# A token mixer without GpSimd: low parts on VectorE, conditioning sums on TensorE, dt inside an exponent

## The chip, the cores and the metric

The kernel runs on one core of a Trainium2 chip. A core has TensorE (matrix products into PSUM), VectorE and ScalarE (elementwise work, both reach SBUF and PSUM), GpSimd (elementwise work on SBUF), SyncE (here the issuer of nearly all DMAs) and 16 DMA engines. In the profile they are PE (PEld for its weight loads), DVE, ACT, POOL and SP. Each engine works through its own queue in order; semaphores make one wait for another. The metric is the device time of one execution in microseconds (us).

## The reference

One encoder layer on 256 tokens of width 1024: a token mixer and a top-4-of-32 mixture of experts, each normalised before and after and modulated by a conditioning vector. Cut to what matters here:

```python
mod = silu(c) @ w_ada + b_ada                       # 6 x 1024: shift, scale, gate, twice
h = rmsnorm(res) * (1 + scale_m) + shift_m
proj = h @ w_in                                     # 1024 x 5664: q, k, v, z, xbc, dt
# 16 attention heads: three dilated windows, ALiBi, mixed by their softmax sums
attn = softmax(q k^T / 8 - slope * |i - j| + log(count of windows)) v
# SSD, 16 heads, forward and backward: xbc through a convolution over 5 tokens and silu
dt = softplus(dt_raw + dt_bias); a_cum = cumsum(dt * -exp(a_log))
y = (C B^T * exp(a_cum_l - a_cum_s) * dt_s, masked) @ xs + d_skip * xs
y = rmsnorm(y * silu(z))
res = res + gate_m * rmsnorm([attn, y] @ w_out)
# experts: 32 x (1024 x 2048 and 1024 x 1024), top 4 of each token
```

## The kernel before, in words

One function writes every engine's queue in program order; nothing is reordered behind it, so the order of the code is the order of each queue.

**Weights.** All weights come as 1 MB blocks through a ring of buffers (`RING`, 7 at first, more as other pools close), in one fixed list `loads`: 8 blocks of `w_ada` for the first modulation, then 22 blocks of `w_in` (256 columns each) with 16 further blocks of `w_ada` between them from the seventh on, 8 blocks of `w_out`, then 12 per expert. `consumed(i)` says that a block is no longer needed; its buffer then takes the next load, issued on SyncE's queue.

**Products in two parts.** The large products of the mixer are made with fp32 numbers split into a high part and a low part. `split(i, a)` does this for half a block (128 x 1024): ScalarE copies the half into `wh` (rounding it), then `wl = w - wh` (L383) is made, on GpSimd where `on_pool` says so (57 halves), else on VectorE (3). `ahead` calls it two halves before use. `mm3` then makes three matmuls, high by high, high by low, low by high. `unit` is one half block: 24 matmuls of 256 columns (L391).

**The projection loop** runs over n = 0 to 21, a block of `w_in` each, two units per n. The columns come in the order: six blocks for the convolution, four z, four q, then k and v in turn. After each unit stand the conditioning work (`mod_half`, from n = 5) and steps of a background list (`bg`), whose number `PACE` sets: the cumulative sums, then the SSD heads in eight pairs j (`ssd_bg`, from n = 7), then the attention heads in eight pairs (`att_bg`, from n = 14, as k and v arrive). A part of `bg` stands in the middle of a unit.

**Conditioning.** The other five rows of `mod` are eight groups of 512 columns. For each group VectorE multiplies 8 slices of `w_ada` (128 x 512) by a column of silu(c) and adds them up (`macc`, L354 and L356); then `mod_sum` sums over the partitions with four matmuls in a 128 x 32 form (L366), which put group g into row g of each quarter of a PSUM tile (`pssq`).

**SSD.** `ssd_decay(h)` builds a head's exponents in PSUM (L556 to L559: at each position the cumulative sum, plus a mask of -1e30), ScalarE takes exp with the bias `natok` (L563), and VectorE multiplies by dt and by C B^T (`cbm`, L565, four pieces per head: 256, 128, 128, 256 columns). `ssd_merge` adds forward and backward on the two diagonal blocks (L575), `ssd_out` multiplies with the inputs (L583), `ssd_fin` squares and splits the result (L593, L595).

**Attention.** `att_scores(j)` makes the scores of two heads (L640), VectorE adds the table of distances and takes the row maximum in one instruction (L652), L655 negates it, ScalarE takes exp and the row sums (L657). `att_norm(j)` divides by the sums (L664, L666 on VectorE), `att_T(j)` turns them (L680 on TensorE, L682), `att_out(j)` multiplies with v (L691). In `att_bg` the steps are: scores of j, normalising of j - 1 and output of j - 2, turning of j - 1.

**After the loop** come the output projection (16 halves of `w_out`, again `ahead` and `mm3`), beside it the splitting of the expert biases (`bias_parts`, L299, L300, loads `bgu` in four chunks), the router and the experts.

Of the kernel before, what the change touches and what calls it, by code (L numbers as in the profile page):

```python
# [40 lines left out]
MIXC = dict(le=128, ones=128, ge=128, dist=384, lnc=384)  # L41


def make_consts():
# [13 lines left out]
        dist=dist, lnc=np.where(count > 0, np.log(np.maximum(count, 1)), NEG))  # L58
# [16 lines left out]
def tile_hybrid_block(  # L75
# [136 lines left out]
    dist, lnc = mcx[:, 0:384], mcx[:, 384:768]  # L212
# [18 lines left out]
    one31 = mi.tile([P, 63], F32, name="one31")  # L231
    dve.memset(one31, 0.0)
    dve.memset(one31[:, 31:32], 1.0)
# [53 lines left out]
    act.activation(csT, colv[:, 0:8], AF.Silu)  # L287
    dve.tensor_copy(ident_b, ident)
# [56 lines left out]
    def mod_half(i, a):  # L345

        w = wt[W_MOD[i]].rearrange("p (k n) -> p k n", k=4)
        if i % 2 == 0 and a == 0:
            macc[i // 2] = mb.tile([P, 512], F32, name="macc", tag="macc", bufs=2)
        acc = macc[i // 2]  # L350
        for kk in range(2 * a, 2 * a + 2):
            k = 4 * (i % 2) + kk
            if k == 0:
                dve.tensor_scalar(acc, w[:, kk, :], csT[:, 0:1], None, op0=OP.mult)  # L354
            else:
                dve.scalar_tensor_tensor(acc, w[:, kk, :], csT[:, k:k + 1], acc, op0=OP.mult, op1=OP.add)  # L356
# [3 lines left out]
    macc = {}  # L360

    def mod_sum(g):

        acc = macc.pop(g)
        for b in range(4):
            pe.matmul(pssq[32 * b:32 * b + 32, 128:256], one31[:, 31 - g:63 - g], acc[:, 128 * b:128 * b + 128],  # L366
                      start=(g == 0), stop=True, tile_position=(0, 32 * b), skip_group_check=True)
# [7 lines left out]
    def on_pool(i, a):  # L375
        return W_IN[order[1]] <= i < W_OUT[6] or (i, a) == (W_OUT[6], 0)

    def split(i, a, pl=None, bufs=3):
# [4 lines left out]
        (pool if on_pool(i, a) else dve).tensor_sub(lo.bitcast(F32R), src, hi)  # L383
# [118 lines left out]
    def cumulate():  # L502
# [25 lines left out]
        dve.tensor_scalar(natok, pt2[:, 0:64].rearrange("p (t n) -> p t n", t=2), -1.0, None, op0=OP.mult)  # L528
# [16 lines left out]
    BLK = ((0, 256, 0, 0, 0), (384, 128, 1, 0, 128), (256, 128, 0, 1, 0), (512, 256, 1, 1, 0))  # L545
    mt = {}

    def ssd_decay(h):
# [82 lines left out]

    slopes = [2.0 ** (-8.0 * (h + 1) / HEADS) for h in range(HEADS)]
    pts = {}

    def att_scores(j):
# [8 lines left out]
        for q in range(2):  # L644
            h = 2 * j + q
            tb = mb.tile([P, 384], F32, name="tb", tag="tb", bufs=2)
            dve.scalar_tensor_tensor(tb, dist, -slopes[h], lnc, op0=OP.mult, op1=OP.add)
            sc = scs[:, 512 * q:512 * q + 512].rearrange("p (t k) -> p t k", t=2)
            st = mb.tile([P, 8], F32, name="st", tag="st", bufs=4)
            for t in range(2):  # L650
                o = 128 - 128 * t
                dve.tensor_tensor_reduce(out=sc[:, t, :], in0=pair[q][:, 256 * t:256 * t + 256],  # L652
                                         in1=tb[:, o:o + 256], scale=1.0, scalar=-3.0e38,
                                         op0=OP.add, op1=OP.max, accum_out=st[:, t:t + 1])
            dve.tensor_scalar(st[:, 2:4], st[:, 0:2], -1.0, None, op0=OP.mult)  # L655
            for t in range(2):
                act.activation(sc[:, t, :], sc[:, t, :], AF.Exp, bias=st[:, 2 + t:3 + t],  # L657
# [681 lines left out]
```

## Time and profile before

| | us |
|---|---|
| median of 3 runs | 1361.26 (1360.2 to 1363.12) |
| the profiled execution, its own time | 1363.41 |
| its span, first to last instruction | 1361.3 |
| start, to the second unit | 0 to 43.3 |
| first blocks: convolution, dt | 43.3 to 91.0 |
| n = 6, 7 | 91.0 to 115.7 |
| n = 8 to 13, SSD | 115.7 to 189.9 |
| n = 14, 15, SSD | 189.9 to 222.7 |
| n = 16 to 21, attention | 222.7 to 300.9 |
| output projection | 300.9 to 360.0 |
| norm, router, selection | 360.0 to 391.5 |
| experts and end | 391.5 to 1361.3 |

The stages are cut at the first matmul of a unit, or of the first expert. [...] A row of a wait names who waited for whose result. Busy time of VectorE includes the time in which a started instruction stands still.

### The profile page before, as it was taken

The numbers are of one execution on the slowest core, as the hardware profiler recorded it, in microseconds if no ns is written. First come the engines' busy times: TensorE is split into PE (matmuls) and PEld (weight loads), VectorE is DVE, ScalarE is ACT, GpSimd is POOL, SyncE is SP. The second block draws the span as 40 slices with busy tenths as digits, with TensorE's granted clock in tenths as the row PEclk, the third lists the DMA queues.
The fourth block names the chain that finished last, engine by engine and source line by source line (L and its number), as shares of the span: only waits on it lengthen the run. The fifth ranks groups of instructions, "written<-read, shape, count | busy, mean of one in ns | idle before, by whom it ended". The sixth has DMA issues, their size and how long they took to land. (4 is left out here: it accounts for less than half of the span.)

```text
span 1361.3 us, 16342 instructions
## 1 busy us (share of the span) xinstructions
PE 1174.9 (86%) x6394; PEld 587.1 (43%) x6394; DVE 456.7 (34%) x866; ACT 262.9 (19%) x582; POOL 168.6 (12%) x91
## 2 busy tenths in 40 slices
PE   3877776889879999999995999999998999999996
PEld 1776665676633333333342333333333333333332
DVE  0799998875711111211110111112111111111113
ACT  1645344543311000110010110001100001110001
POOL 0555443346300000000000000000000000000000
PEclk9889887989889999999997999999999899999998
DMA  8855644456669999999997999999999999999992
GB/s 312 258 175 194 196 155 136 162 184 267 264 248 413 414 413 415 414 414 413 413 417 306 415 415 413 415 413 415 414 413 409 415 415 414 416 415 413 413 385 101
DMA packets 113466, 465.96 MB, mean 342 GB/s; under 512 B 10955, under 2 KB 34163, under 8 KB 79507
## 3 DMA queue, kind: packets, MB, share of 16 engines
q1 hardware_dynamic: 112576, 462.39, 86.1%
q8 instruction: 106, 1.74, 0.5%
q10 hardware_dynamic: 723, 1.33, 0.3%
q14 instruction: 61, 0.50, 0.1%
HBM read 462.65 MB, written 1.05 MB: 341 GB/s over the span
## 5 line engine op out<-in xcount | busy, mean ns | idle before, releaser
L1118 PE MATMUL pq_u<-w,xg 128*64 128x512 f32 x1024 | 275.0, 595 | 2.1 <-issue 2.1
L1118 PE MATMUL pq_g<-w,xg 128*64 128x512 f32 x1024 | 274.5, 596 | 1.5 <-issue 1.0
L1156 PE MATMUL pq_u<-w,aT 128*64 128x512 f32 x1008 | 226.8, 595 | 2.3
L1129 DVE TENSOR_SCALAR g<-pq_g 128x512 f32<-128x512 f32 (+1 forms) x33 | 22.6, 683 | 474.7 <-PE pq_g L1118 271.1
L383 POOL TENSOR_TENSOR wl<-w,wh 128x1024 fp32r<-128x1024 f32 x57 | 145.6, 2560 | 137.9 <-ACT wh L382 133.1
L1130 ACT ACTIVATE sg<-g 128x512 f32<-128x512 f32 (+1 forms) x33 | 20.6, 623 | 723.4 <-DVE g L1129 701.4
L1118 PEld LDWEIGHTS pq_u<-w,xg 128*64 128x64 f32 x1024 | 77.5, 138 | 144.7 <-issue 142.5
L1118 PEld LDWEIGHTS pq_g<-w,xg 128*64 128x64 f32 x1024 | 76.8, 138 | 133.1 <-issue 120.1
L1156 PEld LDWEIGHTS pq_u<-w,aT 128*64 128x64 f32 x1008 | 70.6, 137 | 136.8 <-issue 124.2
L1228 DVE COPY y<-pq_u 128x512 f32<-128x512 f32 x31 | 21.5, 692 | 228.5 <-PE pq_u L1156 227.6
L391 PE MATMUL ps_pj<-hh,wh 128*128 128x256 f32 x296 | 94.0, 317 | 4.3 <-DVE hh L449 3.4
L391 PE MATMUL ps_pj<-hh,wl 128*128 128x256 f32 x296 | 89.9, 304 | 7.4 <-POOL wl L383 7.4
L391 PE MATMUL ps_pj<-hl,wh 128*128 128x256 f32 x296 | 89.7, 303 | 0.0
L827 POOL TENSOR_TENSOR rows<-kc,gp 128x1024 f32<-128x1024 f32 x1 | 1.9, 1895 | 699.9 <-PE o L1074 699.9
L356 DVE SCALAR_TENSOR_TENSOR macc<-w,csT,macc 128x512 f32<-128x512 f32 x56 | 80.9, 1445 | 1.3
L1039 PEld LDWEIGHTS pq_m<-sel,xt 128*128 128x128 f32 x544 | 64.8, 196 | 24.8 <-issue 24.0
L1039 PE MATMUL pq_m<-sel,xt 128*128 128x128 f32 (+1 forms) x544 | 71.0, 285 | 0.0
L1042 ACT ACTIVATE xg<-pq_m,modT,g 128x128 f32<-128x128 f32 x128 | 48.2, 456 | 108.2 <-PE pq_m L1039 108.2
L382 ACT ACTIVATE wh<-w 128x1024 fp32r<-128x1024 f32 x60 | 63.4, 1057 | 29.3 <-issue 8.5
L1167 PE MATMUL o<-y,sT 64*128 64x512 f32 x256 | 65.6, 615 | 1.6 <-DVE y L1304 1.6
L391 PEld LDWEIGHTS ps_pj<-hh,wh 128*128 128x128 f32 x296 | 62.7, 212 | 9.1 <-issue 7.6
L391 PEld LDWEIGHTS ps_pj<-hh,wl 128*128 128x128 f32 x296 | 62.3, 211 | 8.2 <-POOL wl L383 8.2
(302 smaller groups left out, 1148.5 us busy)
## 6 DMA issues: line engine op xcount, KB each, us to landing
w<-in_w_gate_up_dram SPq DMA_DIRECT2D x256, 1024.0 KB, 19.1
w<-in_w_down_dram SPq DMA_DIRECT2D x127, 1024.0 KB, 20.0
w<-in_w_ada_dram SPq DMA_DIRECT2D x24, 1024.0 KB, 5.2
w<-in_w_in_dram SPq DMA_DIRECT2D x22, 1024.0 KB, 13.6
w<-in_w_out_dram SPq DMA_DIRECT2D x8, 1024.0 KB, 5.0
xt<-in_x_dram ACTq DMA_DIRECT2D x1, 1024.0 KB
w<-in_w_down_dram SPq DMA_DIRECT2D x2, 512.0 KB
out_dram<-xt SPq DMA_DIRECT2D x4, 256.0 KB, 2.2
```

Source lines behind the costliest of these rows:

```text
L356: dve.scalar_tensor_tensor(acc, w[:, kk, :], csT[:, k:k + 1], acc, op0=OP.mult, op1=OP.add)
L382: act.activation(hi.bitcast(F32R), src, AF.Copy)
L383: (pool if on_pool(i, a) else dve).tensor_sub(lo.bitcast(F32R), src, hi)
L391: pe.matmul(out_ap, u, v, start=first and i == 0, stop=last and i == 2, skip_group_check=True)
L1039: pe.matmul(p[:, w * i:w * i + w], res[:, t, k * 128:(k + 1) * 128], sel[:, t], start=(t == 0), stop=(t == 1))
L1042: act.activation(xg[:, k], p[:, w * i:w * i + w], AF.Identity, bias=m_shift[:, k:k + 1], scale=g1[:, 8 + k:9 + k])
L1118: pe.matmul(dst[cs * q:cs * q + cs, 0:w], xg[:, k], weight(k, o, w), start=False, stop=(k == KD - 1), tile_position=(0, cs * q), skip_grou ...
L1129: dve.tensor_scalar(g, pg, 7.0, None, op0=OP.min)
L1130: act.activation(s, g, AF.Sigmoid, scale=1.702)
L1156: pe.matmul(py[cs * q:cs * q + cs, 0:w], a4[:, k % nj, k // nj, :], weight(KD + k, w * q, w), start=(k == 0), stop=(k == KD - 1), tile_pos ...
L1167: pe.matmul(oacc[t][hf], sT[64 * q:64 * q + 64, 128 * t:128 * t + 128], y[64 * q:64 * q + 64, :], start=False, stop=False, tile_position=( ...
L1228: dve.tensor_copy(y, py)
```

## The change

- `split`: every low part is made on VectorE; `on_pool` is gone.
- `mod_half`: the sums over `w_ada` are made on TensorE, straight from the weight block, 8 matmuls of 128 columns in the 128 x 32 form for each half block; `cs31` holds each column of silu(c) between zeros, so that the group's sums fall into its row. `macc`, `mod_sum` and their calls are gone; the block is released when TensorE has read it.
- `cumulate`: log(dt) is taken (at least 1e-37) and added to `natok`, so that exp(bias + ...) holds the factor dt. `ssd_decay` ends with the exponentials; `ssd_merge` adds the diagonal blocks and then multiplies by C B^T in one instruction of 512 columns.
- Attention: q is scaled by -0.125 and the table negated; the row minimum of the negated scores is the bias of the exponential, whose scale is -1; L655 is gone. `att_norm` multiplies on ScalarE.

```diff
+    cs31 = mi.tile([P, KD, 63], F32, name="cs31")
+    pool.memset(cs31, 0.0)
...
+    dve.tensor_copy(cs31[:, :, 31:32], csT[:, :, None])
...
     def mod_half(i, a):
...
-        acc = macc[i // 2]
+        g = i // 2
         for kk in range(2 * a, 2 * a + 2):
             k = 4 * (i % 2) + kk
-            if k == 0:
-                dve.tensor_scalar(acc, w[:, kk, :], csT[:, 0:1], None, op0=OP.mult)
-            else:
-                dve.scalar_tensor_tensor(acc, w[:, kk, :], csT[:, k:k + 1], acc, op0=OP.mult, op1=OP.add)
+            for b in range(4):
+                pe.matmul(pssq[32 * b:32 * b + 32, 128:256], cs31[:, k, 31 - g:63 - g], w[:, kk, 128 * b:128 * b + 128],
+                          start=(i == 0 and k == 0), stop=True, tile_position=(0, 32 * b), skip_group_check=True)
...
-        (pool if on_pool(i, a) else dve).tensor_sub(lo.bitcast(F32R), src, hi)
+        dve.tensor_sub(lo.bitcast(F32R), src, hi)
...
-        dve.tensor_scalar(natok, pt2[:, 0:64].rearrange("p (t n) -> p t n", t=2), -1.0, None, op0=OP.mult)
+        dve.tensor_scalar(natok, ddt[:, :, 0:32], 1e-37, None, op0=OP.max)
+        act.activation(natok, natok, AF.Ln)
+        dve.scalar_tensor_tensor(natok, pt2[:, 0:64].rearrange("p (t n) -> p t n", t=2), -1.0, natok,
+                                 op0=OP.mult, op1=OP.add)
...
-        for o, n, t, dr, lo in BLK:
-            dve.scalar_tensor_tensor(ee[:, o:o + n], ee[:, o:o + n], ddt[:, t, 16 * dr + h:16 * dr + h + 1],
-                                     cbm[:, h // 8, 256 * t + lo:256 * t + lo + n], op0=OP.mult, op1=OP.mult)
...
+        both = bass.AP(tensor=m.tensor, offset=m[:, 0:1].offset, ap=[list(m.ap[0]), [512, 2], [1, 256]])
+        dve.tensor_tensor(out=both, in0=both, in1=cbm[:, h // 8, :].rearrange("p (t n) -> p t n", t=2), op=OP.mult)
...
-            dve.scalar_tensor_tensor(tb, dist, -slopes[h], lnc, op0=OP.mult, op1=OP.add)
+            dve.scalar_tensor_tensor(tb, dist, slopes[h], nlc, op0=OP.mult, op1=OP.add)
...
-                                         in1=tb[:, o:o + 256], scale=1.0, scalar=-3.0e38,
-                                         op0=OP.add, op1=OP.max, accum_out=st[:, t:t + 1])
-            dve.tensor_scalar(st[:, 2:4], st[:, 0:2], -1.0, None, op0=OP.mult)
+                                         in1=tb[:, o:o + 256], scale=1.0, scalar=3.0e38,
+                                         op0=OP.add, op1=OP.min, accum_out=st[:, t:t + 1])
             for t in range(2):
-                act.activation(sc[:, t, :], sc[:, t, :], AF.Exp, bias=st[:, 2 + t:3 + t],
+                act.activation(sc[:, t, :], sc[:, t, :], AF.Exp, bias=st[:, t:t + 1], scale=-1.0,
                                accum_out=st[:, 4 + t:5 + t])
...
-                dve.tensor_scalar(sc[:, t, :], sc[:, t, :], st[:, 6 + t:7 + t], None, op0=OP.mult)
+                act.activation(sc[:, t, :], sc[:, t, :], AF.Copy, scale=st[:, 6 + t:7 + t])
...
-        if n > ADA_AT and (n - ADA_AT) % 2 == 0 and n - ADA_AT <= len(W_MOD):
-            mod_sum((n - ADA_AT) // 2 - 1)
```

On VectorE, in the SSD stage (one n; `ee` is a head's mask, `w_956` a conditioning block, `yt` the output of a pair), the queue before reads:

```order
L565 SCALAR_TENSOR_TENSOR ee<-ee,ddt,cbm 128x256
L565 SCALAR_TENSOR_TENSOR ee<-ee,ddt,cbm 128x128 x2
L565 SCALAR_TENSOR_TENSOR ee<-ee,ddt,cbm 128x256
L356 SCALAR_TENSOR_TENSOR macc<-w_956,csT,macc 128x512 x2
L565 SCALAR_TENSOR_TENSOR ee<-ee,ddt,cbm 128x256
L565 SCALAR_TENSOR_TENSOR ee<-ee,ddt,cbm 128x128 x2
L565 SCALAR_TENSOR_TENSOR ee<-ee,ddt,cbm 128x256
L575 TENSOR_TENSOR ee<-ee 128x2x128
L356 SCALAR_TENSOR_TENSOR macc<-w_956,csT,macc 128x512 x2
L586 SCALAR_TENSOR_TENSOR yt<-blk_c,dsk,ps_t 128x256
L587 TENSOR_TENSOR yt<-yt,blk_z 128x256
L575 TENSOR_TENSOR ee<-ee 128x2x128
```

and in the changed kernel, in the same stage (`w_1020` is a block of `w_in`, `wl` its low part):

```order
L368 TENSOR_TENSOR wl<-w_1020,wh 128x1024
L584 SCALAR_TENSOR_TENSOR blk_c<-yt,ghalf,blk_z 128x256
L561 TENSOR_TENSOR ee<-ee 128x2x128
L563 TENSOR_TENSOR ee<-ee,cbm 128x2x256
L368 TENSOR_TENSOR wl<-w_1020,wh 128x1024
L574 SCALAR_TENSOR_TENSOR yt<-blk_c,dsk,ps_t 128x256
```

The eight mask products and the conditioning products are gone; a low part stands before and behind the merge of a head, which now carries the product with C B^T.

On ScalarE, in the attention stage (`sc` are scores, `wh` the high part of a half block), before, from one pair's exponentials (L657) to the turned scores (L682):

```order
L382 ACTIVATE wh<-w_2007 128x1024
L682 ACTIVATE prT<-ps_t 128x512 x2
L657 ACTIVATE sc,st<-sc,st 128x256 x4
L739 ACTIVATE vt<-ps_pj 128x2x256
L382 ACTIVATE wh<-w_2149 128x1024
L694 ACTIVATE blk_q<-ps_pj 128x256
L682 ACTIVATE prT<-ps_t 128x512 x2
```

and after:

```order
L367 ACTIVATE wh<-w_2071 128x1024
L670 ACTIVATE prT<-ps_t 128x512 x2
L645 ACTIVATE sc,st<-sc,st 128x256 x4
L727 ACTIVATE vt<-ps_pj 128x2x256
L367 ACTIVATE wh<-w_2217 128x1024
L654 ACTIVATE sc<-sc,st 128x256 x4
L682 ACTIVATE blk_q<-ps_pj 128x256
L670 ACTIVATE prT<-ps_t 128x512 x2
```

Four normalising instructions (L654) now stand on ScalarE between a pair's exponentials and the copies of the turned scores.

On TensorE the eight matmuls of a conditioning half block now stand behind each unit, here between the last of its 24 matmuls and the output of an SSD pair:

```order
L376 MATMUL ps_pj<-hl,wh 128x256
L376 MATMUL ps_pj<-hh,wl 128x256
L352 MATMUL pssq<-w_986,cs_123 32x128 x8
L571 MATMUL ps_t<-ee,xtk 64x256 x4
L376 MATMUL ps_pj<-hh,wh 128x256
```

Before, four such matmuls from `macc` stood there once in two n.

## Rows read from the trace of the kernel before

**Rows 1.** Windows by stage: us, busy time by engine (instructions), PE clock, DMA share, GB/s

```profile
43.30:91.00 47.70, 41.01 (x326) 38.69 (x325) 38.38 (x57) 23.72 (x36) 28.99 (x14) 0.96 0.68 214
91.00:115.70 24.70, 16.55 (x122) 15.00 (x120) 24.45 (x35) 11.38 (x20) 10.98 (x5) 0.92 0.61 199
115.70:189.90 74.20, 57.98 (x452) 51.57 (x449) 73.60 (x109) 35.31 (x75) 37.76 (x18) 0.89 0.53 171
189.90:222.70 32.80, 24.44 (x173) 19.20 (x169) 30.29 (x48) 11.64 (x29) 12.59 (x8) 0.84 0.50 161
222.70:300.90 78.20, 64.54 (x465) 54.89 (x461) 61.36 (x146) 37.84 (x94) 30.67 (x12) 0.89 0.45 149
300.90:360.00 59.10, 49.87 (x237) 38.23 (x234) 39.41 (x60) 21.88 (x33) 35.45 (x17) 0.98 0.67 259
```

**Rows 2.** Single source lines: duration ns minimum/median/maximum, first and last start us, shapes

```profile
L356 DVE SCALAR_TENSOR_TENSOR macc<-w,csT,macc x56: 736/752/2935, 93.9 to 290.6; 128x512 f32<-128x512 f32 x56
L428 DVE SCALAR_TENSOR_TENSOR ctmp<-halo,colv,ctmp x48: 471/473/2650, 61.3 to 113.5; 128x256 f32<-128x256 f32 x48
L666 DVE TENSOR_SCALAR sc<-sc,st x32: 346/353/2534, 231.6 to 315.1; 128x256 f32<-128x256 f32 x32
L383 POOL TENSOR_TENSOR wl<-w,wh x57: 2375/2443/3012, 44.5 to 349.8; 128x1024 fp32r<-128x1024 f32 x57
L383 DVE TENSOR_TENSOR wl<-w,wh x3: 1201/1210/1225, 36.3 to 357.4; 128x1024 fp32r<-128x1024 f32 x3
```

**Rows 3.** Timeline near 50 us, GpSimd and VectorE: start us, us, what

```profile
50.38 2.42 POOL L383 TENSOR_TENSOR wl<-w,wh 128x1024 fp32r<-128x1024 f32 x1 [0.43 <-ACT wh L382]
50.50 2.39 DVE L483 SCALAR_TENSOR_TENSOR vt<-vt 128x64 f32<-128x64 f32 x1
```

**Rows 4.** Waits of TensorE, 43.3 to 360: us in total, times, longest us

```profile
PE ps_bc L556 <- ACT ee L563: 16.7, 12, 4.4
PE ps_t L680 <- DVE sc L666: 14.6, 5, 5.0
...
PE ps_bc L391 <- DVE wl L383: 4.4, 1, 4.4
```

**Rows 5.** Timeline near 260 us, VectorE and TensorE, idle time before in brackets

```profile
257.23 8.84 DVE L356 SCALAR_TENSOR_TENSOR macc<-w,csT,macc 128x512 f32<-128x512 f32 x4
271.02 1.94 PE L680 MATMUL ps_t<-kc,sc 128*128 128x128 f32 x8 [4.97 <-DVE sc L666]
```

**Rows 6.** Groups by line on VectorE, 0 to 400: busy us, mean ns | idle before

```profile
L356 DVE SCALAR_TENSOR_TENSOR macc<-w,csT,macc 128x512 f32<-128x512 f32 x56 | 80.9, 1445 | 1.3
L565 DVE SCALAR_TENSOR_TENSOR ee<-ee,ddt,cbm 128x256 f32<-128x256 f32 (+1 forms) x64 | 41.0, 702 | 0.6 <-ACT ee L563 0.6
L666 DVE TENSOR_SCALAR sc<-sc,st 128x256 f32<-128x256 f32 x32 | 15.8, 536 | 0.6
L300 DVE CAST bias<-bgu 96x512 bf16<-96x512 f32 (+2 forms) x12 | 12.9, 1074 | 9.4 <-DMA bgu<-in_b_gate_up_dram 9.1
L911 DVE TENSOR_TENSOR xtk<-xtk,gbm 128x512 f32<-128x512 f32 x4 | 2.7, 685 | 0.2 <-ACT junk L908 0.2
```

**Rows 7.** Timeline of TensorE around two sums over partitions (L366)

```profile
135.77 0.66 PE L366 MATMUL pssq<-macc,one 128*32 128x128 f32 x8
136.36 0.58 PE L391 MATMUL ps_pj<-hh,wh 128*128 128x256 f32 x1
276.64 0.42 PE L366 MATMUL pssq<-macc,one 128*32 128x128 f32 x8
277.00 0.39 PE L391 MATMUL ps_pj<-hh,wh 128*128 128x256 f32 x1
```

**Rows 8.** Groups by line on ScalarE: busy us, mean ns | idle before

```profile
L595 ACT ACTIVATE blk_z<-yt,ghalf 128x256 fp32r<-128x256 f32 x8 | 3.9, 492 | 0.0
L563 ACT ACT_TABLE_LOAD x1 | 1.3, 1283 | 0.0
```

**Rows 9.** Window at the first expert's first matmuls, columns as in rows 1

```profile
390.00:395.00 5.00, 3.52 (x12) 1.25 (x14) 0.00 (x0) 0.00 (x0) 0.00 (x0) 0.50 0.01 3
```

More of the change, by code (lines that the diff above doesn't have):

```diff
@@ L40 @@
 KEEPB = dict(lt=128, e3=NE, up=128, low=128)
-MIXC = dict(le=128, ones=128, ge=128, dist=384, lnc=384)
+MIXC = dict(le=128, ones=128, ge=128, dist=384, nlc=384)
 def make_consts():
@@ L57, in make_consts @@
         blk=row // 32 == np.arange(4)[None, :],
-        dist=dist, lnc=np.where(count > 0, np.log(np.maximum(count, 1)), NEG))
+        dist=dist, nlc=np.where(count > 0, -np.log(np.maximum(count, 1)), -NEG))
     def pack(names):
@@ L211, in tile_hybrid_block @@
     mcx = mb.tile([P, 768], F32, name="mcx")
-    dist, lnc = mcx[:, 0:384], mcx[:, 384:768]
+    dist, nlc = mcx[:, 0:384], mcx[:, 384:768]
     qT, kT, zT, cvx = {}, {}, {}, {}
@@ L230, in tile_hybrid_block @@
     arow = mi.tile([P, 32], F32, name="arow")
-    one31 = mi.tile([P, 63], F32, name="one31")
-    dve.memset(one31, 0.0)
-    dve.memset(one31[:, 31:32], 1.0)
+    cs31 = mi.tile([P, KD, 63], F32, name="cs31")
+    pool.memset(cs31, 0.0)
     dsk = mx.tile([P, 8], F32, name="dsk")
@@ L347, in mod_half @@
         w = wt[W_MOD[i]].rearrange("p (k n) -> p k n", k=4)
-        if i % 2 == 0 and a == 0:
-            macc[i // 2] = mb.tile([P, 512], F32, name="macc", tag="macc", bufs=2)
-        acc = macc[i // 2]
+        g = i // 2
         for kk in range(2 * a, 2 * a + 2):
             k = 4 * (i % 2) + kk
-            if k == 0:
-                dve.tensor_scalar(acc, w[:, kk, :], csT[:, 0:1], None, op0=OP.mult)
-            else:
-                dve.scalar_tensor_tensor(acc, w[:, kk, :], csT[:, k:k + 1], acc, op0=OP.mult, op1=OP.add)
+            for b in range(4):
+                pe.matmul(pssq[32 * b:32 * b + 32, 128:256], cs31[:, k, 31 - g:63 - g], w[:, kk, 128 * b:128 * b + 128],
+                          start=(i == 0 and k == 0), stop=True, tile_position=(0, 32 * b), skip_group_check=True)
         if a:
             consumed(W_MOD[i] + 1)
[L360 to L367, printed above, removed]
     ptx = [ps("bc", 2), ps("bc", 2), ps("pj", 3), ps("pj", 3)]
@@ L373, in tile_hybrid_block @@
             pe.transpose(ptx[k // 2][:, o:o + 128], xn[:, t, k * 128:(k + 1) * 128], ident)
-    def on_pool(i, a):
-        return W_IN[order[1]] <= i < W_OUT[6] or (i, a) == (W_OUT[6], 0)
     def split(i, a, pl=None, bufs=3):
@@ L541, in xs_tok @@
         act.activation(xtk[:, t, 512 * hf:512 * hf + 512], p, AF.Copy)
-    BLK = ((0, 256, 0, 0, 0), (384, 128, 1, 0, 128), (256, 128, 0, 1, 0), (512, 256, 1, 1, 0))
+    BLK = ((0, 256, 0, 0), (384, 128, 1, 0), (256, 128, 0, 1), (512, 256, 1, 1))
     mt = {}
@@ L560, in ssd_decay @@
         ee = big("ee")
-        for o, n, t, dr, lo in BLK:
+        for o, n, t, dr in BLK:
             src = 0 if n == 256 else 256
             act.activation(ee[:, o:o + n], pb[dr][:, src:src + n], AF.Exp, bias=natok[:, t, h + 16 * dr:h + 16 * dr + 1])
-        for o, n, t, dr, lo in BLK:
-            dve.scalar_tensor_tensor(ee[:, o:o + n], ee[:, o:o + n], ddt[:, t, 16 * dr + h:16 * dr + h + 1],
-                                     cbm[:, h // 8, 256 * t + lo:256 * t + lo + n], op0=OP.mult, op1=OP.mult)
         mt[h] = ee
@@ L752, in evac @@
                 qT[j + i] = blk("q")
-                dve.tensor_scalar(qT[j + i], v3[:, i], 0.125, None, op0=OP.mult)
+                dve.tensor_scalar(qT[j + i], v3[:, i], -0.125, None, op0=OP.mult)
             yield
```

## The prediction

> **What bounds the kernel now.** I read the table of stages first. The span has three parts: a start of 43 us that the loads pace, the token mixer up to about 391 us, and the 32 experts. Only the mixer is edited. In its input projection after the convolutions, 91.0 to 300.9 us, VectorE is busy 24.45 + 73.60 + 30.29 + 61.36 = 189.7 of 209.9 us, 90%; TensorE is idle 8.15 + 16.22 + 8.36 + 13.66 = 46.4 us and runs at a mean granted clock between 0.84 and 0.92 [rows 1]. [...]
>
> Why VectorE is full I read from minimum, median and maximum of single lines. The conditioning sum (L356) takes 752 ns in the median and 2935 at most, a convolution tap (L428) 473 and 2650; the longest exceed the median by about one GpSimd low part, 2443 ns [rows 2]. The timeline shows the mechanism: at 50.38 us GpSimd starts a low part of 2.42 us, at 50.50 VectorE starts an operation on 64 columns that ends only when the low part does, after 2.39 us [rows 3]. So an instruction of VectorE that meets a low part waits it out.
>
> Who waits for VectorE comes from the waits. TensorE waits 16.7 us for the exponentials of the SSD mask and 14.6 us for normalised attention scores [rows 4]. One case in full: four products of the conditioning sum hold VectorE from 257.23 for 8.84 us, the next scores come late, and TensorE stands 4.97 us before L680 at 271.02 [rows 5]. VectorE's backlog sets the mixer's pace, TensorE pays.
>
> **The change, part by part.** *Conditioning sums leave VectorE*: 56 products, 80.9 us of its time, of which 56 x 0.752 = 42 us is work and the rest waiting for GpSimd [rows 2, 6]. *The SSD mask*: 64 three-operand products, 41.0 us, become 16 plain products of 512 columns. The nearest row is L911 (512 columns, two SBUF inputs), 685 ns: 16 x 0.685 = 11.0 us [rows 6]. *Low parts come to VectorE*: 57 at the 1.21 us that three of them take there already, 69 us in all [rows 2]; between 91.0 and 300.9 us it is 32 (two for each of 16 steps), 38.7 us. VectorE's sum there: 189.7 - 80.9 - 41.0 + 38.7 + 11.0 = 117.5 us, 56% of the old stretch, before the blocked time on what stays is taken off. It stops being the bound.
>
> *Conditioning sums come to TensorE*: 32 half blocks of 8 matmuls each, which is two groups of four in the form of L366; L366 itself (8 groups) goes. A group takes 277.00 - 276.64 = 0.36 us from its start to the next matmul at full clock, 136.36 - 135.77 = 0.59 at half clock, the switch out of and into the 128 x 128 form included [rows 7]. So 64 - 8 = 56 groups add 20.2 us, or 33.0 if all fell at half clock. I take 20.2, since these groups stand right behind 24 matmuls of a unit, where the engine has been running. Nothing hides them: TensorE is in order. This is the price of the change. TensorE now also waits itself for each conditioning block's load; the DMA share of 0.45 to 0.61 in these stages [rows 1] leaves room, so I cost that at nothing; a late block would stop TensorE by as much as it is late.
>
> *Normalising goes to ScalarE*: 32 multiplications of VectorE (15.8 us, median 353 ns) become ScalarE instructions. The nearest row is L595, 256 columns with a per-partition scale, 492 ns: 15.7 us [rows 2, 6, 8]. ScalarE is busy 37.8 of 78.2 us in that stage [rows 1], so 24 of them (11.8 us) fit; but they now stand behind the exponentials of the next pair, in the chain scores, exponentials, normalising, transposes that already ends at L680. [...]
>
> *Small ones*: the logarithm of dt adds an instruction to VectorE, one to ScalarE and two table loads of 1.28 us [rows 8], once, between 60 and 91 us, where ScalarE is busy 23.7 of 47.7 us [rows 1]: 0, at most 3 us if the masks wait for it. The sign changes drop 16 tiny instructions; a GpSimd fill and a copy of 8 columns fall into the start, which loads pace.
>
> *Order.* Nothing is scheduled anew, but each low part now stands in VectorE's queue behind whatever waits there. In the projection it is wanted two units later, each 24 matmuls plus about 0.7 us of conditioning, so a wait of a few us is covered. Two places are tight. Near 50 us the dt chain now starts behind a low part (1.21 us, itself behind ScalarE's high part), and TensorE's transposes wait for that chain. In the output projection the bias casts (L300) wait 9.1 us for their DMA [rows 6], and low parts that GpSimd made meanwhile now queue behind them.
>
> **The sum**, stage by stage. 43.3 to 91.0: VectorE is busy 38.4 of 47.7 us, it gets some eleven low parts (13.3 us) and loses blocked time of about that size; I take 0, bounds -4 and +5 (idle is 6.7). 91.0 to 300.9: with VectorE at 56% I let 70% of the idle go, 32.5 us; the rest are latencies of chains such as the one before L680. The clock goes with the idle: the stages with the smallest idle share, 43.3 to 91.0 and 300.9 to 360.0, have 0.96 and 0.98 [rows 1]. All of the 48 us worked off at 2.4 GHz would give 24 us, I take 60%, 14.4. Less 20.2 for the new matmuls: 26.7. 300.9 to 360.0: of 9.2 us idle the 4.4 us wait for a late low part on VectorE goes [rows 4]; I take 4, bounds -5 (the bias DMA) and +9. Together 30.7, say 31 us.
>
> What the mixer gains, the experts pass on: weights stop arriving at 390 to 395 us (DMA share 0.01), because every ring buffer is full before the first expert's matmuls free one [rows 9]. The expert stage starts earlier with the same stock. The profiled execution took 1363.4 us, so it would be 1332; the runs' median is 2 us below it, and 1361.3 - 31 gives **1330**.
>
> **Rivals.** *(a) TensorE fully busy.* All 46.4 us idle and 24 us of slow clock go: 46.4 + 24 - 20.2 = 50 us, with 7 more from the ends: 1304. For it: VectorE and ScalarE both fall well under TensorE. Against: some waits are chains across four engines that no spare capacity shortens.
>
> *(b) The queue takes half back.* Low parts stand behind waiting instructions and normalising behind exponentials; only half of the idle and the slow clock go: 23 + 12 - 20 = 15 us, nothing at the ends: 1346. For it: 14.6 us of the waits are at L680, whose chain gets longer on ScalarE. Against: the longest of them is the conditioning sum's doing, and that is gone.
>
> *(c) Slower: TensorE is already the pacer and its new work is simply added.* If the waits are latencies rather than backlog, none goes, and 56 groups cost 20.2 us, at half clock 33: 1381 to 1394. It decides as soon as idle and slow clock give back less than 20 us together. Against it: VectorE's idle time in 115.7 to 189.9 us is 0.6 of 74.2 us, which is no latency. [...]
>
> *(d) No effect: the time is lost again before or in the expert stage.* An earlier start with an emptier ring would make the experts wait for weights at the end; 1361. Against: the loads stand still for several us before the first expert.
>
> **Numbers.** Forecast 0.55; (a) 0.16; (b) 0.17; (c) 0.06; (d) 0.06. The predicted time is that of the forecast. The range leaves out (c), (d) and the far half of (a): 1306 to 1350. Measurement can tell 0.2% (2.7 us) from no change: faster 0.89, same 0.05, slower 0.06.
>
> **What would show it.** VectorE's busy share in the projection near 55 to 60%, its products without a tail near 2.7 us, no GpSimd low parts; 64 groups of conditioning matmuls, 0.36 us each; TensorE idle there 10 to 18 us and granted clock about 0.95; experts' matmuls starting near 361 us instead of 391, and the last stage as long as before. I am wrong if TensorE still waits over 25 us there, if low parts on VectorE take clearly more than 1.21 us, or if the first expert starts earlier and the end does not.

## The result, and the profile after

The changed kernel takes 1320.3 us in the median (1319.6 to 1321.95, four runs), the kernel before beside it 1362.19; the ratio is 0.969, with an interval of 0.9669 to 0.9711. That is 42 us less; the forecast was 31 less, 1330 us, with a range of 1306 to 1350. The profiled execution has a span of 1320.2 us and took 1321.95.

| stage, us | before | after |
|---|---|---|
| first blocks: convolution, dt | 47.7 | 45.3 |
| n = 6, 7 | 24.7 | 16.9 |
| n = 8 to 13, SSD | 74.2 | 55.9 |
| n = 14, 15, SSD | 32.8 | 21.9 |
| n = 16 to 21, attention | 78.2 | 75.2 |
| output projection, to its last matmul | 65.6 | 61.3 |
| norm, router, selection | 25.4 | 26.1 |
| experts and end | 969.4 | 974.4 |

The output projection ends here with its last matmul (at 366.5 us before, 319.7 after) and the experts begin with the first matmul on their weights (391.9 and 345.7 us); the table before cuts at 360.0 and 391.5.

The windows by stage after, cut like those of [rows 1] and with the same columns (the clock is the mean granted share of TensorE's full clock); the fifth row is attention, the last the experts with the product of their biases just before:

```profile
43.20:88.50 45.30, 40.70 (x358) 38.40 (x356) 34.30 (x75) 27.26 (x41) 1.17 (x3) 0.99 0.73 231
88.50:105.40 16.90, 16.47 (x181) 14.91 (x177) 13.84 (x24) 10.57 (x19) 0.00 (x0) 1.00 0.83 274
105.40:161.30 55.90, 55.55 (x619) 48.26 (x616) 35.02 (x58) 35.99 (x75) 3.75 (x4) 1.00 0.70 227
161.30:183.20 21.90, 21.82 (x226) 17.70 (x224) 16.62 (x28) 11.91 (x29) 3.65 (x4) 1.00 0.67 208
183.20:258.40 75.20, 66.89 (x599) 55.10 (x597) 35.85 (x101) 47.35 (x118) 0.00 (x0) 0.95 0.47 164
...
345.30:1320.20 974.90, 882.39 (x4394) 343.61 (x4394) 163.26 (x334) 96.64 (x246) 4.66 (x4) 0.98 0.97 394
```

In the three stages from 88.5 to 183.2 us TensorE is idle for 0.43 + 0.35 + 0.08 = 0.9 of 94.7 us, at full clock throughout: there it sets the pace, and VectorE is busy 13.84 + 35.02 + 16.62 = 65.5 us. What is left stands in the attention stage: 75.20 - 66.89 = 8.3 us idle, and a mean clock of 0.95. The lines answering to [rows 2] and to two prices of the sum, in that view:

```profile
L413 DVE SCALAR_TENSOR_TENSOR ctmp<-halo,colv,ctmp x48: 476/481/485, 61.4 to 99.4; 128x256 f32<-128x256 f32 x48
L368 DVE TENSOR_TENSOR wl<-w,wh x60: 1201/1226/2132, 36.2 to 313.0; 128x1024 fp32r<-128x1024 f32 x60
L563 DVE TENSOR_TENSOR ee<-ee,cbm x16: 691/692/693, 110.9 to 178.2; 128x512 f32<-128x512 f32 x16
L654 ACT ACTIVATE sc<-sc,st x32: 492/494/508, 193.2 to 272.8; 128x256 f32<-128x256 f32 x32
```

The convolution taps have lost their tail (485 ns at most, 2650 before); low parts (1226 ns), mask products (692) and the normalising instructions (494) cost what nearest rows had said (1210, 685, 492). TensorE's waits from 43.2 to 330 us, answering to [rows 4] (us in total, times, longest):

```profile
PE ps_t L668 <- ACT sc L654: 8.8, 5, 4.1
PE ps_t L465 <- DVE vt L462: 2.7, 1, 2.7
...
PE ps_bc L545 <- ACT ee L552: 0.3, 2, 0.2
```

The wait for the SSD exponentials is gone (16.7 to 0.3 us); that for normalised scores stays at 8.8 us where it was 14.6, now behind ScalarE. Of the two tight places one shows: TensorE waits 2.7 us for the dt chain (L462), 0.6 before. The other doesn't: the bias casts wait 3.1 us for their DMA, not 9.1.

### The profile page after: what moved, and what is told of

It is laid out like the page before. It is cut to its first block, busy times and chain, and to the rows that moved or that the text cites. A ratio compares the mean times of both kernels' runs of the same rounds, so it can differ in the third digit from the quotient of the medians.

```text
span 1320.2 us, 17110 instructions
## 1 busy us (share of the span) xinstructions
PE 1172.1 (89%) x6842; PEld 580.0 (44%) x6842; DVE 360.5 (27%) x763; ACT 279.1 (21%) x617; POOL 24.9 (2%) x35
## 5 line engine op out<-in xcount | busy, mean ns | idle before, releaser
L1104 PE MATMUL pq_g<-w,xg 128*64 128x512 f32 x1024 | 270.9, 601 | 4.1 <-DMA w<-in_w_gate_up_dram 3.1
L1104 PE MATMUL pq_u<-w,xg 128*64 128x512 f32 x1024 | 269.2, 598 | 2.3 <-issue 2.3
L376 PE MATMUL ps_pj<-hh,wh 128*128 128x256 f32 x296 | 89.6, 303 | 3.6 <-DVE hh L434 3.6
L368 DVE TENSOR_TENSOR wl<-w,wh 128x1024 fp32r<-128x1024 f32 x60 | 74.7, 1246 | 59.0 <-ACT wh L367 58.9
L376 PE MATMUL ps_pj<-hh,wl 128*128 128x256 f32 x296 | 85.6, 289 | 2.4 <-DVE wl L368 2.4
L376 PE MATMUL ps_pj<-hl,wh 128*128 128x256 f32 x296 | 85.5, 289 | 0.0
L1214 DVE COPY y<-pq_u 128x512 f32<-128x512 f32 x31 | 21.4, 692 | 228.4 <-PE pq_u L1142 227.5
L1025 PEld LDWEIGHTS pq_m<-sel,xt 128*128 128x128 f32 x544 | 64.8, 195 | 24.0 <-issue 23.2
L1153 PE MATMUL o<-y,sT 64*128 64x512 f32 x256 | 65.6, 615 | 1.6 <-DVE y L1290 1.6
L376 PEld LDWEIGHTS ps_pj<-hh,wh 128*128 128x128 f32 x296 | 58.3, 197 | 9.5 <-issue 9.0
L376 PEld LDWEIGHTS ps_pj<-hh,wl 128*128 128x128 f32 x296 | 57.9, 196 | 2.9 <-DVE wl L368 2.8
L376 PEld LDWEIGHTS ps_pj<-hl,wh 128*128 128x128 f32 x296 | 58.0, 196 | 0.1
L1100 PE MATMUL pq_g<-bias,kb 96*64 96x512 bf16 (+1 forms) x68 | 13.7, 406 | 46.0 <-DVE y L1214 26.4
```

Source lines behind the costliest of these rows:

```text
L368: dve.tensor_sub(lo.bitcast(F32R), src, hi)
L376: pe.matmul(out_ap, u, v, start=first and i == 0, stop=last and i == 2, skip_group_check=True)
L1025: pe.matmul(p[:, w * i:w * i + w], res[:, t, k * 128:(k + 1) * 128], sel[:, t], start=(t == 0), stop=(t == 1))
L1100: pe.matmul(dst[cs * q:cs * q + cs, 0:w], kbv["e3"][0:3 * NE, e:e + 1].to_broadcast([3 * NE, cs]), bias3[:, o:o + w], start=True, stop=Fal ...
L1104: pe.matmul(dst[cs * q:cs * q + cs, 0:w], xg[:, k], weight(k, o, w), start=False, stop=(k == KD - 1), tile_position=(0, cs * q), skip_grou ...
L1153: pe.matmul(oacc[t][hf], sT[64 * q:64 * q + 64, 128 * t:128 * t + 128], y[64 * q:64 * q + 64, :], start=False, stop=False, tile_position=( ...
```

## The experiments

Each kernel was timed beside the kernel before on its chip. The changed kernel itself took 1320.3 us in one such series and 1324.26 in another, so kernels of different series are compared by their ratios too. A is VectorE standing still while GpSimd works, the theory of the prediction. Line numbers in rows are those of the kernel that was run.

**Low parts back on GpSimd**, the rest as changed:

```diff
+    def on_pool(i, a):
+        return W_IN[order[1]] <= i < W_OUT[6] or (i, a) == (W_OUT[6], 0)
...
-        dve.tensor_sub(lo.bitcast(F32R), src, hi)
+        (pool if on_pool(i, a) else dve).tensor_sub(lo.bitcast(F32R), src, hi)
```

> The changed kernel with the low parts of 57 halves back on GpSimd; all else as changed. VectorE then has 32 x 1.23 = 39 us less work of its own between the seventh block of w_in and the last, about 71 us. Theory A (a low part on GpSimd blocks VectorE, so its place matters in itself): VectorE's busy time there stays above 100 us because of blocked instructions, products of 0.48 us reach 2.5 us again, TensorE idles 15 to 30 us, and the time is 1328 to 1342 us. Rival B (only VectorE's own load counts, and 71 us is even less): 1316 to 1321 us.

1330.9 us, ratio 0.9786 (0.9763 to 0.9809): 10.6 us of the 42 go, 13 by the ratios. VectorE's groups by line (busy us, mean ns | idle before) show the blocking:

```profile
L416 DVE SCALAR_TENSOR_TENSOR ctmp<-halo,colv,ctmp 128x256 f32<-128x256 f32 x48 | 37.4, 847 | 8.8 <-ACT ctmp L413 8.7
L578 DVE TENSOR_TENSOR yt<-yt,blk_z 128x256 f32<-128x256 f32 x8 | 14.8, 1851 | 0.3
```

A tap takes 847 ns in the mean instead of about 480 with its work unchanged: the tail is back with GpSimd's low parts. The first blocks last 51.7 us instead of 45.3 and the next three stages 2.7 to 5.7 more each; but attention is shorter, 67.4 us instead of 75.2. That speaks for low parts on GpSimd in that one stage, and is followed up below. The input projection in this run, with the columns of [rows 1], and one wait of TensorE:

```profile
94.30:268.50 174.20, 164.15 (x1617) 137.88 (x1613) 85.39 (x177) 104.80 (x241) 84.64 (x41) 0.97 0.58 194
PE ps_pj L379 <- POOL wl L371: 4.6, 3, 2.0
```

The time fell into the range of theory A, two of its signs did not: VectorE is busy 85.39 us there and not over 100, and TensorE is idle 10.05 us and not 15 to 30. Some of that idle time isn't blocking either: TensorE waits 4.6 us directly for low parts of GpSimd, which takes twice as long for one (2443 ns in [rows 2], 1226 on VectorE). The next run has blocking without that wait.

**GpSimd busy for nothing.** The changed kernel, low parts on VectorE, and beside each of those of `w_in` from its second block on, to the attention's end, a subtraction on GpSimd that nobody reads (42 of them):

```diff
         dve.tensor_sub(lo.bitcast(F32R), src, hi)
+        if W_IN[order[1]] <= i < W_OUT[8]:
+            pool.tensor_sub(bias3.bitcast(F32)[:, 0:1024], src[0:96], hi[0:96])
```

> The changed kernel, and beside each of the 42 low parts of w_in from the second block on, GpSimd makes the same subtraction once more on 96 partitions into a buffer that nobody reads before it is written anew. VectorE's and TensorE's own work is that of the changed kernel. Theory A (blocking): VectorE's 110 us of work in the projection get up to 32 x 2.4 = 78 us of blocked time on top, TensorE idles again, 1332 to 1352 us. Rival B (load alone counts): GpSimd's work is beside the path, 1319 to 1323 us.

1372.95 us, ratio 1.0081 (1.0063 to 1.0098): 52 us over the changed kernel, where theory A had 32 at most, and slower than the kernel before. In this run VectorE does the same work as in the changed kernel. VectorE's groups by line:

```profile
L368 DVE TENSOR_TENSOR wl<-w,wh 128x1024 fp32r<-128x1024 f32 x59 | 85.1, 1447 | 43.8 <-ACT wh L367 43.5
L415 DVE SCALAR_TENSOR_TENSOR ctmp<-halo,colv,ctmp 128x256 f32<-128x256 f32 x48 | 36.5, 829 | 0.0
L563 DVE TENSOR_TENSOR ee<-ee 128x256 f32<-128x256 f32 x16 | 18.5, 1158 | 0.2 <-ACT ee L554 0.2
```

And GpSimd's, the unread subtraction:

```profile
L370 POOL TENSOR_TENSOR bias<-w,wh 96x1024 f32<-96x1024 f32 x42 | 126.0, 3000 | 118.4 <-ACT wh L367 102.3 <-issue 14.0 <-POOL bias L370 1.2
```

The merge of a head's diagonal blocks (L563 here, L561 in the changed kernel) grows from 420 to 1158 ns, a tap to 829; GpSimd's instruction, on three quarters of the partitions of a low part, takes 3000 ns in the mean, more than the 2443 in [rows 2]: each holds up the other. A rival that knows only the load of VectorE falls. Nobody reads these results, but the subtraction reads the weight block, whose buffer is free only after it. SyncE does wait for that before it issues loads, and yet ScalarE's wait for blocks of `w_in`, up to 400 us, is as short as in the changed kernel (1.6 us there):

```profile
SPq L142 <- POOL bias L370: 36.7, 15, 6.1
ACT wh L367 <- DMA w<-in_w_in_dram: 1.4, 1, 1.4
```

So the loads came in time. GpSimd's own work for the SSD also stands behind the unread subtractions now, and ScalarE waits 6.2 us for it, never in the changed kernel. That is small beside 52 us; the rest is A by itself.

**Low parts alone**: the kernel before, with every low part on VectorE and nothing else changed.

```diff
-        (pool if on_pool(i, a) else dve).tensor_sub(lo.bitcast(F32R), src, hi)
+        dve.tensor_sub(lo.bitcast(F32R), src, hi)
```

> The kernel before with one edit: every low part on VectorE. Its own work between the seventh and the last block of w_in is then 144 us without blocked time, and 39 us of low parts, 183 us in a stage that took 210. Theory A (blocking by GpSimd costs VectorE about 65 us there): products of 0.75 us lose their tail of 2.9 us, the stage shortens to about 185 to 200 us, 1335 to 1352 us. Rival B (only the load counts; 190 + 39 = 229 us): slower, 1375 us or more.

1333.79 us, ratio 0.9795 (0.977 to 0.982): 29 us, a little more than the best I had expected, though VectorE takes 69 us of work over. Up to 7.4 of these 29 us can be another thing than blocking, TensorE's direct waits for low parts of GpSimd in the kernel before:

```profile
PE ps_pj L391 <- POOL wl L383: 7.4, 4, 2.3
```

**Conditioning alone**: the kernel before, with the sums over `w_ada` on TensorE and the low parts left on GpSimd.

```diff
...
-            if k == 0:
-                dve.tensor_scalar(acc, w[:, kk, :], csT[:, 0:1], None, op0=OP.mult)
-            else:
-                dve.scalar_tensor_tensor(acc, w[:, kk, :], csT[:, k:k + 1], acc, op0=OP.mult, op1=OP.add)
+            for b in range(4):
+                pe.matmul(pssq[32 * b:32 * b + 32, 128:256], cs31[:, k, 31 - g:63 - g], w[:, kk, 128 * b:128 * b + 128],
+                          start=(i == 0 and k == 0), stop=True, tile_position=(0, 32 * b), skip_group_check=True)
...
```

> The kernel before with one edit: the conditioning sums on TensorE. VectorE loses 46 us of work (85 us with what blocked it), low parts stay on GpSimd, TensorE gets 16 us. Theory A: the low parts now block other instructions of VectorE, so only part is regained: 1338 to 1352 us. Rival C (the conditioning sums are the whole gain): 1318 to 1328 us.

1332.69 us, ratio 0.9774 (0.9739 to 0.981): 30 us, between the 1338 us that theory A had at least and the 1328 that rival C had at most. Both pieces give about 70% of the whole alone, and 59 us if added, against 42 measured together: they stand in for one another. How, one window over the input projection after the convolutions shows, with the columns of [rows 1]. The kernel before:

```profile
91.00:300.90 209.90, 163.52 (x1199) 140.66 (x1197) 189.71 (x334) 96.17 (x217) 91.99 (x41) 0.89 0.50 165
```

Low parts alone:

```profile
87.10:270.50 183.40, 153.53 (x1198) 132.47 (x1197) 161.85 (x359) 94.75 (x214) 6.33 (x8) 0.93 0.56 184
```

Conditioning alone:

```profile
91.80:266.40 174.60, 162.10 (x1618) 137.00 (x1612) 113.12 (x267) 96.03 (x217) 86.39 (x41) 0.97 0.58 196
```

And the changed kernel:

```profile
88.50:258.40 169.90, 160.73 (x1617) 135.98 (x1613) 101.33 (x210) 105.83 (x240) 7.41 (x8) 0.98 0.61 201
```

With low parts alone VectorE stays busy 161.85 of 183.40 us, 88%: it still paces the stage and has only less to do in it. A product of the conditioning sum takes 764 ns in the mean there, not 1445 [rows 6]. With conditioning alone it falls to 65%, and TensorE's idle time from 46.4 to 12.5 us. Then TensorE sets the pace, and low parts on VectorE, with the smaller pieces of the change, find only 174.6 - 169.9 = 4.7 us to take here. Most of the rest of what they bring lies at the ends, where there is no conditioning work to remove: with conditioning alone the first blocks last 48.5 and the output projection 64.3 us, about as before (47.7 and 65.6), in the changed kernel 45.3 and 61.3.

**Conditioning back on VectorE**, the rest as changed:

```diff
...
-            for b in range(4):
-                pe.matmul(pssq[32 * b:32 * b + 32, 128:256], cs31[:, k, 31 - g:63 - g], w[:, kk, 128 * b:128 * b + 128],
-                          start=(i == 0 and k == 0), stop=True, tile_position=(0, 32 * b), skip_group_check=True)
+            if k == 0:
+                dve.tensor_scalar(acc, w[:, kk, :], csT[:, 0:1], None, op0=OP.mult)
+            else:
+                dve.scalar_tensor_tensor(acc, w[:, kk, :], csT[:, k:k + 1], acc, op0=OP.mult, op1=OP.add)
...
```

> The changed kernel with the conditioning sums back on VectorE (64 products) and the sums over partitions by 32 matmuls. VectorE gets 56 x 0.75 + 8 x 0.48 = 46 us, 156 us of work in a stage of 170; TensorE loses about 16 us. Theory A (freed of GpSimd, VectorE can carry them): the two nearly cancel, 1314 to 1328 us. Rival C (the gain is the conditioning sums' leaving VectorE): 1335 us or more, with TensorE idle over 25 us in the projection.

1330.45 us, ratio 0.9782 (0.9757 to 0.9808): 10 us slower than the changed kernel, 12.5 by the ratios. That is over the range of theory A and below that of rival C, and TensorE's idle time in the projection, 24.39 us, nearly reaches the 25 that rival C named:

```profile
88.30:265.80 177.50, 153.11 (x1199) 131.03 (x1197) 143.84 (x276) 106.06 (x241) 7.37 (x8) 0.94 0.59 194
```

So VectorE, free of GpSimd, carries the sums only at a loss. The SSD stages n = 8 to 13 are even 2.2 us shorter than with the new matmuls (53.7 against 55.9); attention is 7.2 longer, 82.4, and its wait grows:

```profile
PE ps_t L680 <- ACT sc L666: 13.5, 7, 4.6
```

So the conditioning matmuls, 15.7 us of TensorE, pay in the attention stage, not in the SSD stages. The output projection is longer here too, 64.8 us against 61.3, but part of that can be chance of a run: in the seven other profiles with these matmuls and no low parts of `w_out` on GpSimd it takes 61.1 to 63.1. That low parts and conditioning products then stand ahead of the attention's work on VectorE is the likely reading; it was argued, not tried by itself.

**The mask as before**, with its four dt products per head, the rest as changed:

```diff
...
+        for o, n, t, dr, lo in BLK:
+            dve.scalar_tensor_tensor(ee[:, o:o + n], ee[:, o:o + n], ddt[:, t, 16 * dr + h:16 * dr + h + 1],
+                                     cbm[:, h // 8, 256 * t + lo:256 * t + lo + n], op0=OP.mult, op1=OP.mult)
...
-        dve.tensor_tensor(out=both, in0=both, in1=cbm[:, h // 8, :].rearrange("p (t n) -> p t n", t=2), op=OP.mult)
```

> The changed kernel with the SSD mask as before: four three-operand products per head on VectorE with dt, no logarithm in the bias. VectorE gets 27 - 11 = 16 us more in the SSD stages (35 of 56 us busy in the changed kernel, now 45 to 48). Theory A (VectorE has room there, nothing blocks it): TensorE's idle in these stages stays under 4 us, 1319 to 1325 us. Rival (this piece carries a third of the gain): 1330 us or more.

1322.83 us, ratio 0.9707 (0.9683 to 0.9731): 2.5 us more in the median, but its interval overlaps that of the changed kernel, and the SSD stages are as long as there (55.9 and 21.4). VectorE has room for the 11 us more: the 64 products take 22.0 us here, the 16 plain ones 11.1 in the changed kernel.

**The division back on VectorE**, the rest as changed:

```diff
-                act.activation(sc[:, t, :], sc[:, t, :], AF.Copy, scale=st[:, 6 + t:7 + t])
+                dve.tensor_scalar(sc[:, t, :], sc[:, t, :], st[:, 6 + t:7 + t], None, op0=OP.mult)
```

> The changed kernel with the division of the scores back on VectorE (32 times 0.35 us in place of 0.49 us on ScalarE). Theory D (the wait that is left, 8.8 us of TensorE before the transposes of the scores, is ScalarE's queue: normalising stands behind the next pair's exponentials): these waits fall to 2 to 5 us and the time to 1313 to 1318 us. Rival (the wait is the latency from scores to sums, whichever engine divides): 1319 to 1322 us.

1321.05 us, ratio 0.9708 (0.9692 to 0.9724): no difference. TensorE's wait, 8.8 us before, nearly keeps its size and changes its name:

```profile
PE ps_t L668 <- DVE sc L654: 7.5, 4, 3.5
```

The attention stage of this profile is 1.8 us shorter, 73.4, which the time doesn't show. So ScalarE's 494 ns against VectorE's 350 decide little; most of what the chain waits for is ahead of the division.

**The last low parts of the loop on GpSimd**: the changed kernel, with the ten low parts of n = 17 to 21 (those made in the attention stage) on GpSimd. Timed twice, the second time with the changed kernel once more on the same chip, and with the division back on VectorE as a third.

```diff
-        dve.tensor_sub(lo.bitcast(F32R), src, hi)
+        (pool if W_IN[order[17]] <= i < W_OUT[8] else dve).tensor_sub(lo.bitcast(F32R), src, hi)
```

> The changed kernel with the low parts of the last five blocks of w_in (10 halves, made while attention runs) on GpSimd, all others on VectorE. With all 57 there the attention stage took 67.4 us, in the changed kernel 75.1, while every other stage was longer by 2 to 6. Theory E (in that stage a low part on VectorE stands ahead of the scores of a pair, and the chain from scores to transposes paces TensorE): the stage falls to 67 to 70 us, the others keep their times, 1312 to 1317 us. Rival (the 7.7 us were shifted from other stages, as the pairs of heads start later there): 1319 to 1323 us.

> The changed kernel itself once more, on the same chip as the next two, so that these are compared with it and not only with the kernel before; and a second look at the lengths of its stages. Ratio to the kernel before 0.969 expected, as measured (0.9669 to 0.9711). If the five microseconds that the expert stage lost belong to the changed kernel, the stage is 974 to 975 us again; if they are chance of a run, anything from 969 to 976.

> The changed kernel with the ten low parts of the last five input blocks on GpSimd, once more and beside the changed kernel. Theory E (the attention chain waits behind low parts on VectorE): faster than the changed kernel by 4 to 7 us, attention stage 67 against 75 us. Rival (the lower time came from that chip): no difference to the changed kernel on the same chip beyond 2.7 us.

> As the run before, and the division by the sums back on VectorE. With the low parts away VectorE has room in the attention stage and its division is shorter (350 against 494 ns), but an instruction that meets one of GpSimd's low parts stands still up to 2.4 us. Theory F (the chain ends at ScalarE's queue once the low parts are away): 1 to 4 us faster than the run before. Rival (the blocked ones eat what the shorter instruction gives, or the chain has slack by then): within 1 us of it.

The first time 1315.13 us, ratio 0.9646 (0.9619 to 0.9673). On one chip then: the changed kernel 1324.26, 0.9709 (0.9689 to 0.9729); with ten low parts on GpSimd 1314.44, 0.9646 (0.9626 to 0.9665); with the division moved as well 1313.2, 0.9633 (0.9614 to 0.9653). The ten low parts are worth 9.8 us on this chip (8.6 by the ratios; 4 to 7 were expected), where the intervals lie apart, and 5 us by the first comparison, across series, where the intervals overlap. The attention stage, first time:

```profile
183.70:250.80 67.10, 64.19 (x598) 52.20 (x596) 25.11 (x91) 46.69 (x118) 24.01 (x10) 1.00 0.51 184
```

And TensorE's wait for normalised scores in it:

```profile
PE ps_t L668 <- ACT sc L654: 2.8, 3, 1.3
```

67.1 us instead of 75.2 (the second time 67.1 against 76.3), at full clock, and the wait for normalised scores falls from 8.8 to 2.8 us. So the chain scores, exponentials, division, transposes was held up by low parts ahead of it in VectorE's queue. One likely reason that blocking costs little there is in the last section: the addition of the distances isn't blocked. Where the division stands makes 1.2 us, which the intervals don't separate. With one or two lines changed this is the fastest version of all that were run: 1313 to 1315 us.

**The kernel before once more**, for its expert stage, unchanged, so without a diff:

> The kernel before once more, for a second look at its expert stage, which took 969.4 us in the first profile against 974.4 and 976.5 in two profiles of the changed kernel. If the stage got longer by the change (an earlier start with an emptier ring, or another cause in the code), it is 969 to 970 us again. If its length is chance of a run, it lies anywhere from 969 to 977, likely near 973. Ratio to the kernel before 1.000 within its interval.

1362.6 us, ratio 0.9997 (0.9986 to 1.0007), and 969.6 us for the expert stage. So in two profiles each the stage takes 969.4 and 969.6 us in the kernel before, 974.4 and 976.5 in the changed one.

## Why the prediction was right, and which terms were off

**The bound, and the mechanism.** VectorE's backlog, fed by standing still beside GpSimd, set the mixer's pace. The standing still is shown by unread work on GpSimd; that the backlog set the pace, by the two pieces alone, each of which shortens VectorE's queue and gains some 30 us. That an instruction of VectorE that meets a low part waits it out was said too widely: in the kernel before the nine that read PSUM and started during a low part ran through, in 419 to 472 ns (last section). VectorE's share in the projection is 101.33 of 169.9 us, 60%, where 55 to 60 was said. That fits by luck in part: the sum had 117.5 us, since it left the normalising and the sign changes on VectorE, and took its share of the old, longer stretch.

**The idle term was too small.** I let 70% of 46.4 us go, 32.5, and kept the rest as latency of chains. It is 37.2 (9.2 us left, where 10 to 18 was the sign), since only attention kept such a chain; in the SSD stages nothing of it was latency. On those stages rival (a), TensorE fully busy, was right.

**The clock term was too small.** No run shows the 2.4 GHz of this term, and a unit's matmuls do not take twice as long at the lower level. What the trace of the kernel before shows is two levels of the granted clock, 1.00 and 0.50 (0.50 from 137 to 139 us, 1.00 from 140 to 145), and by the means of [rows 1] 2 x (24.7 x 0.08 + 74.2 x 0.11 + 32.8 x 0.16 + 78.2 x 0.11) = 48 us of the projection at 0.50. There a unit's 256-column matmuls start 213 ns apart in the median, at 1.00 120 ns, so all 48 us would have given 48 x 93 / 213 = 21 us and not 24. Of the 48 us at the lower level about 75.2 x 0.05 x 2 = 7.5 are left, so by this pace, as an estimate, the clock gave back (48 - 7.5) x 93 / 213 = 17.7 us instead of 14.4. The stages with idle time gone are at 1.00.

**The price of conditioning was too high.** TensorE's timeline around one half block:

```profile
122.11 0.64 PE L352 MATMUL pssq<-w,cs 128*32 128x128 f32 x16
122.69 1.08 PE L571 MATMUL ps_t<-ee,xtk 128*64 128x256 f32 x8
```

From its start to the next matmul it takes 0.58 us, as do 28 of the 32 half blocks (behind the other four TensorE waited), not two groups of 0.36 [rows 7]: eight matmuls stand together, and eight take 0.22 us more than four did before the next matmul starts, not 0.36 more. 32 x 0.58 - 8 x 0.36 = 15.7 us instead of 20.2. Together -37.2 - 17.7 + 15.7 = -39.2; measured -40.0. Idle time at the lower level, 4.6 of the 48 us before, stands in both terms, and the pace is that of a unit's matmuls alone, so that the two come so close is luck in part. The forecast for this stretch was -26.7.

**The ends.** 0 was taken for the first blocks: they gained 2.4 us, inside the bounds, although TensorE now waits 2.7 us for the dt chain. Part of it can be chance: in the other profiles of kernels with every low part there on VectorE this stage takes 44.8 to 47.0 us, and 62.8 with unread work beside it. The output projection gained 4.3 where 4 was said, which is luck in part. The wait for the late low part didn't go, it fell from 4.4 to 2.2 us, and idle time in the stage from 9.2 to 7.0; the other 2.1 us are TensorE's busy time (56.37 and 54.28 us), as the mean clock rose from 0.95 to 1.00, a term that had not been counted there.

**Normalising on ScalarE** is no gain, as the costs by instruction said: 494 ns there, 350 on VectorE with the division back, and the same time. That its chain would still end in TensorE's wait for normalised scores was said in rival (b); that this wait hangs on the low parts ahead and not on the division was not. As a whole (b) falls with the 80% of the idle time that went, and (c) since idle time and clock gave back 37.2 + 17.7 us, far over 20.

**Passing the gain on was a little wrong.** The first expert starts 391.9 - 345.7 = 46.2 us earlier, the end comes 41.1 earlier. "The last stage as long as before" failed by 5 us (7 in the second profile), and so the total came nearer to the forecast than the input projection did. It isn't the early start or an emptier ring: in the run with unread GpSimd work the experts start at 395.3 us and take 976.3. Most of it is one place; other experts differ by up to 2.4 us, some longer and some shorter, which nearly cancels. TensorE in the last expert but one, the window of the changed kernel (columns as in [rows 1]):

```profile
1211.30:1218.00 6.70, 4.44 (x16) 1.27 (x14) 0.00 (x0) 0.00 (x0) 0.00 (x0) 0.76 1.02 415
```

The kernel before at the same place:

```profile
1260.50:1267.00 6.50, 6.50 (x34) 2.30 (x34) 0.00 (x0) 0.00 (x0) 0.00 (x0) 1.00 1.02 412
```

And TensorE's wait in that window of the changed kernel:

```profile
PE pq_u L1104 <- issue: 2.3, 1, 2.3
```

TensorE stands 2.3 us for nothing that the trace shows, then goes on at a granted clock of 0.50 (1214.8 to 1218.0 us): the expert takes 32.3 us instead of 28.1. All ten profiles of kernels with the conditioning matmuls in TensorE's stream show 30.2 to 32.5 us there, the four without them (the kernel before twice, low parts alone, conditioning back on VectorE) 28.1 or 28.2. So it goes with these matmuls, though it stands some 960 us behind them; why, stays open, as does the rest of the stage's scatter (two profiles of one version: 975.1 and 972.4; over all kernels 972.4 to 976.5 with these matmuls, 969.4 to 972.9 without). (d) expected a loss in this stage, but of the whole gain.

**The two pieces are not additive**, which the working hides. It counted VectorE's time over all pieces at once, and one figure for the idle time that goes; for each piece alone theory A expected too little gain, and the measured time lay below its range, since both pieces take their gain from the same waits of TensorE.

## What to carry to other kernels

Where VectorE and GpSimd both work on SBUF, look at minimum, median and maximum of single lines: here a tail as long as the other engine's instruction (752 ns in the median and 2935 at most, beside 2443 on GpSimd [rows 2]) said that work moved from VectorE to GpSimd still cost VectorE its time. Stop taking pieces off an engine once another one paces the stage, and price a second piece against the kernel that has the first. A rule on placing work holds by stage: low parts belonged on VectorE beside the SSD and on GpSimd beside attention, and moving ten of them there gave 5 to 10 us more.

## What the runs showed of the hardware that was not expected

Whether VectorE stood still beside GpSimd went with where the instruction read. In the kernel before 59 instructions that read a tensor started on VectorE while a low part ran on GpSimd: the nine with a tensor in PSUM took 419 to 472 ns and ended before it, and of the 50 with all in SBUF 49 ended only after it. GpSimd and VectorE in the timeline of the kernel before, near 166 us (start us, us, what):

```profile
165.46 2.87 POOL L383 TENSOR_TENSOR wl<-w,wh 128x1024 fp32r<-128x1024 f32 x1
165.97 0.47 DVE L586 SCALAR_TENSOR_TENSOR yt<-blk_c,dsk,ps_t 128x256 f32<-128x256 f32 x1
166.47 2.14 DVE L587 TENSOR_TENSOR yt<-yt,blk_z 128x256 f32<-128x256 f32 x1
```

L586, with one of its tensors in PSUM, runs through inside the low part in its usual 0.47 us; L587, with all in SBUF, starts behind it and ends only at 168.61, after the low part (168.33). With 42 unread subtractions on GpSimd the same holds for the instruction that adds the distances to the scores, again with one tensor in PSUM: 422 ns in the mean, as without them.

```profile
L643 DVE CUSTOM_DVE_ANT_0 sc<-ps_bc,tb 128x256 f32<-128x256 f32 x32 | 12.3, 422 | 3.5 <-PE ps_bc L631 1.5
```

Beside the low part L587 takes 2.14 us, the same instruction in the changed kernel 424 ns in the mean. It reads two tensors; an instruction that reads one was held up as well: the division of the scores (L666), a tensor in SBUF times a column of factors, took up to 2534 ns beside low parts against 353 in the median [rows 2].

And both engines paid. With 42 unread subtractions VectorE is busy 246.80 us from the second unit to the end of the output projection, 175.23 in the changed kernel, and the subtractions take 126.0 us where 42 of the shortest (2.37 us) would make 99.5. The kernel is 52 us longer by it, 17.5 of them in the first blocks (62.8 us against 45.3), which the expectation had not counted.
